# RMS norm of 16,384 rows: three loads issued from ScalarE's queue instead of SyncE's

## The chip, the cores and the metric

The kernel runs on one core of a Trainium2 chip. The metric is the device time of one execution in microseconds (us). A profile of one execution gives, beside that time, the span from the program's first instruction to its last, and says for each instruction when it ran and what it waited for. Engines are named as in the profile: PE (TensorE), DVE (VectorE), ACT (ScalarE), POOL (GpSimd) and SP (SyncE, which computes nothing and issues DMAs).

## The reference

```python
def setup_inputs():
    batch, seq, dim = 16, 1024, 512
    return {
        "x": np.random.randn(batch, seq, dim).astype(np.float32),
        "gamma": np.ones(dim, dtype=np.float32),
    }

def reference(x: np.ndarray, gamma: np.ndarray) -> np.ndarray:
    eps = 1e-5
    rms = np.sqrt(np.mean(x ** 2, axis=-1, keepdims=True) + eps)
    return (x / rms * gamma).astype(np.float32)
```

Each of the 16,384 rows of 512 numbers is divided by the root of its mean square and multiplied by gamma. 33.5 MB are read and 33.5 MB are written.

## The kernel before, in words

**Tiles and slots.** The rows are cut into four tiles (0 to 3) of 128 partitions by 32 rows by 512 numbers. A partition's 32 rows lie in one piece in memory, so that half a tile is 32 KB per partition and 4 MB in all. There are three buffers (`slots`, L40) of a whole tile each: tiles 0, 1 and 2 use slots 0, 1 and 2, and tile 3 uses slot 0 again (`slot_of`, L86), once tile 0 has been stored from it. Results are made in place.

**Groups.** Work goes by half tiles: eight groups, named by tile and first row, from (0, 0), (0, 16) to (3, 16) (L76). For each group:

- ACT squares the rows in pieces (L95) into a buffer in PSUM or SBUF, and DVE sums each piece along the row (L96). Tile 0's groups have pieces of 7 and 9 rows; the 9-row squares go to rows 23 to 31 of slot 2, which is still free. The other groups have pieces of 7, 5 and 4 rows.
- `inverse_rms`: ACT takes the square root (L101), DVE the reciprocal (L102).
- POOL multiplies the last 7 rows (6 in the first group, 3 in the last) by the reciprocal and then by gamma (L108, L109). ACT multiplies the others by the reciprocal, one instruction a row (L117), and DVE multiplies those by gamma, all in one instruction (L121).

**Order.** The order is written out by hand (`manual_schedule`, L33): every engine takes its own instructions in the order of the program. The loop at L161 runs one group ahead with the squares: while group k is scaled, the squares of group k+1 are made. In ACT's order one turn is: the next group's first two pieces of squares, the first half of this group's scalings, the third piece of squares, the second half of the scalings, what `transfers` issues, and the square root for the next group. PE only spreads gamma over the partitions at the start (L66).

**Transfers.** All DMAs are issued by SP, in the order of the program, into one queue. An issue that has to wait for something holds every issue behind it. Tile 0 (in three pieces, with gamma between), tile 1 and then tile 2's first half are loaded with no wait. `transfers` (L128), called after each group's last instruction on DVE (L175), issues the rest: tile 2's second half after group (0, 0), which has to wait for the sums of the squares kept in slot 2; after (0, 16) the two stores of tile 0, and the two loads of tile 3, each of which waits until the store of the same rows has landed; one 8 MB store of tile 1 after (1, 16), one of tile 2 after (2, 16), and two 4 MB stores of tile 3, after (3, 0) and (3, 16). `declare_no_dep` (L126) takes away waits of L121 that ACT has already made.

Of the kernel before, what the change touches and what calls it, by code (L numbers as in the profile page):

```python
# [9 lines left out]
def kernel(  # L10
# [6 lines left out]
    nc = tc.nc  # L17
# [12 lines left out]
    xv = xf.rearrange("(t p r) d -> t p r d", p=P, r=R)  # L30
# [9 lines left out]
    slots = [const.tile([P, R, D], fp32, name=f"slot{i}") for i in range(3)]  # L40

    before_scale = []

    def load(t, slot, r0, r1):
        dma = nc.sync.dma_start(out=slots[slot][:, r0:r1], in_=xv[t][:, r0:r1])  # L45
        before_scale.append((slot, r0, r1, dma))

    def store(t, slot, r0, r1):
        dma = nc.sync.dma_start(out=ov[t][:, r0:r1], in_=slots[slot][:, r0:r1])
        before_scale.append((slot, r0, r1, dma))  # L50

    gamma_row = const.tile([1, D], fp32)
    pieces = (0, D)

    load(0, 0, 0, 1)
    load(0, 0, 1, 16)
    for c0, c1 in zip(pieces, pieces[1:]):
        nc.sync.dma_start(out=gamma_row[:, c0:c1], in_=gamma.unsqueeze(0)[:, c0:c1])
    load(0, 0, 16, 32)
    load(1, 1, 0, 16)  # L60
    load(1, 1, 16, 32)
# [26 lines left out]
    def square_sums(ss, t, g, r, m, k):  # L88
        if m == 9:
            sq = slots[2][:, 23:32, :]  # L90
        else:
            home, name, most = ((psum, "sq_psum", 7), (const, "sq_sbuf", 5))[k % 2]
            sq = home.tile([P, most, D], fp32, name=name)
        rows = slots[slot_of[t]][:, g + r : g + r + m, :]
        nc.scalar.activation(out=sq[:, :m], in_=rows, func=AF.Square)  # L95
        nc.vector.tensor_reduce(  # L96
            out=ss[:, r : r + m, 0], in_=sq[:, :m], axis=mybir.AxisListType.X, op=OP.add
        )

    def inverse_rms(ss, n):  # L100
        nc.scalar.activation(out=ss[:, :n, 0], in_=ss[:, :n, 0], func=AF.Sqrt, bias=eps_t, scale=1.0 / D)  # L101
        nc.vector.reciprocal(out=ss[:, :n, 0], in_=ss[:, :n, 0])  # L102
        return ss

    def scale_by_pool(rstd, t, g, n, share):
        part = slots[slot_of[t]][:, g + n - share : g + n, :]
        by_row = rstd[:, n - share : n].to_broadcast([P, share, D])
        nc.gpsimd.tensor_tensor(out=part, in0=part, in1=by_row, op=OP.mult)  # L108
        last = nc.gpsimd.tensor_tensor(  # L109
            out=part, in0=part, in1=gamma_b.to_broadcast([P, share, D]), op=OP.mult  # L110
        )
        before_scale.append((slot_of[t], g + n - share, g + n, last))

    def scale(rstd, t, g, r0, r1):
        x = slots[slot_of[t]]
        for r in range(r0, r1):
            nc.scalar.activation(out=x[:, g + r, :], in_=x[:, g + r, :], func=AF.Copy, scale=rstd[:, r])  # L117

    def times_gamma(t, g, r0, r1):
        part = slots[slot_of[t]][:, g + r0 : g + r1, :]  # L120
        scaled = nc.vector.tensor_tensor(  # L121
            out=part, in0=part, in1=gamma_psum.to_broadcast([P, r1 - r0, D]), op=OP.mult
        )
        for slot, b0, b1, earlier in before_scale:
            if slot == slot_of[t] and b0 < g + r1 and g + r0 < b1:
                tc.declare_no_dep(scaled.ins, earlier.ins, reason="ScalarE waited for it before it scaled these rows")  # L126

    def transfers(t, g):  # L128
        if (t, g) == (0, 0):
            load(2, 2, 0, 16)  # L130
            load(2, 2, 16, 32)
        elif (t, g) == (0, 16):
            store(0, 0, 0, 16)
            store(0, 0, 16, 32)
            load(3, 0, 0, 16)
            load(3, 0, 16, 32)
        elif (t, g) == (1, 16):
            store(1, 1, 0, 32)
        elif (t, g) == (2, 16):
            store(2, 2, 0, 32)  # L140
        elif (t, g) == (3, 0):
            store(3, 0, 0, 16)
        elif (t, g) == (3, 16):
            store(3, 0, 16, 32)

    def pieces_of(group):
        t, g, n, pieces, share = group
        ss = stats.tile([P, 16, 1], fp32, name="ss")
        r = 0
        todo = []  # L150
        for k, m in enumerate(pieces):
            todo.append((ss, t, g, r, m, k))
            r += m
        return ss, todo
# [6 lines left out]
    for k, group in enumerate(groups):  # L161
        t, g, n, pieces, share = group
        mine = n - share
        half = (mine + 1) // 2
        ahead = groups[k + 1 :][:1]
        ss, todo = pieces_of(ahead[0]) if ahead else (None, [])
        scale_by_pool(rstd, t, g, n, share)
        for piece in todo[:2]:
            square_sums(*piece)
        scale(rstd, t, g, 0, half)  # L170
        for piece in todo[2:]:
            square_sums(*piece)
        scale(rstd, t, g, half, mine)
        times_gamma(t, g, 0, mine)
        transfers(t, g)  # L175
        for nxt in ahead:
            rstd = inverse_rms(ss, nxt[2])
# [30 lines left out]
```

## Time and profile before

| what | us |
|---|---|
| median of 3 runs (161.8 to 162.05) | 161.9 |
| the profiled execution, its own time | 161.72 |
| its span, first to last instruction | 159.9 |
| DVE busy, 38 instructions | 112.8 |
| ACT busy, 110 instructions | 109.1 |
| POOL busy, 22 instructions | 102.1 |
| share of 16 DMA engines' span taken by packets | 98.1% |
| mean DMA rate over the span | 420 GB/s |

The page cuts the span into 40 equal slices of 4 us and shows for each engine, and for the DMA engines together, the busy share of a slice in tenths (9 is 90% or more). A row of the order of time gives start, duration, engine, line, operation, what it writes from what it reads, and in brackets how long its engine stood idle before it and what ended that. A row of the waits gives the waiting engine and line, what it waited for, and us in total, times, and the longest; SPq is SP's sequencer, so its waits are those of the DMA queue's issues. A row of the DMA issues gives what is written from what, how often, KB each, and the median time from issue to landing.

### The profile page before, as it was taken

To read this page: it belongs to the slowest core of one execution; us is meant where nothing else is said; L and a number is where in the kernel's file an instruction comes from. 1 tells how busy PE (TensorE), PEld (TensorE's weight loads), DVE (VectorE), ACT (ScalarE), POOL (GpSimd) and SP (SyncE) were. 2 spreads that over 40 slices of the span, in tenths; PEclk is the share of its full clock that TensorE was granted. 3 is DMA by queue.
4 is the path that set the end of the run, shared out by engine and by line. 5 is a ranking of instruction groups with operands and counts; after the bars stand their busy time and mean duration, and the time that the engine had idled before them with its cause. 6 is when DMAs were issued, how large, how long until landed. Compare 5 with 4: busy or idle time off the path is not lost.

```text
span 159.9 us, 258 instructions
## 1 busy us (share of the span) xinstructions
PE 2.0 (1%) x2; PEld 0.5 (0%) x2; DVE 112.8 (71%) x38; ACT 109.1 (68%) x110; POOL 102.1 (64%) x22
## 2 busy tenths in 40 slices
PE   0005000000000000000000000000000000000000
PEld 0001000000000000000000000000000000000000
DVE  0000993797999999999999999999999702950000
ACT  3007906999998899899989989999994297000000
POOL 1000005994079999999999999999999997000000
DMA  5989999999999997999999999997997998999995
GB/s 191 492 369 468 451 393 434 484 393 418 484 410 393 483 426 311 483 393 402 508 402 393 492 426 393 524 475 311 524 459 328 524 426 361 393 459 459 393 426 229
DMA packets 2163, 67.12 MB, mean 420 GB/s; under 512 B 241, under 2 KB 241, under 8 KB 370
## 3 DMA queue, kind: packets, MB, share of 16 engines
q1 hardware_dynamic: 2162, 67.11, 98.1%
q14 instruction: 1, 0.01, 0.0%
HBM read 33.56 MB, written 33.55 MB: 420 GB/s over the span
## 4 chain that ended last, share of the span: by engine, by line
DVE 62%; ACT 18%; DMA 7%; ACTq 0%; SPq 0%; issue 0%
DVE ss L96 36%; DVE slot L121 26%; ACT slot L117 9%; DMA slot<-in_x_dram 7%; ACT slot L95 5%; ACT sq_psum L95 4%; DVE ss L102 1%; ACTq L203 0%; ACT gamma_b L160 0%; SPq L45 0%; ACT ss L101 0%; ACTq L95 0%
## 5 line engine op out<-in xcount | busy, mean ns | idle before, releaser
L108 POOL TENSOR_TENSOR slot<-slot,ss 128x3584 f32<-128x3584 f32 (+2 forms) x8 | 45.0, 5625 | 31.8 <-DVE ss L102 31.8
L96 DVE TENSOR_REDUCE ss<-sq_psum 128x7 f32<-128x3584 f32 (+1 forms) x14 | 44.5, 3176 | 19.5 <-ACT sq_psum L95 19.5
L109 POOL TENSOR_TENSOR slot<-slot,gamma_b 128x3584 f32<-128x3584 f32 (+2 forms) x8 | 56.9, 7112 | 0.6
L117 ACT ACTIVATE slot<-slot,ss 128x512 f32<-128x512 f32 x77 | 48.5, 707 | 4.9 <-DVE ss L102 4.9
L121 DVE TENSOR_TENSOR slot<-slot,gamma_psum 128x4608 f32<-128x4608 f32 (+2 forms) x8 | 42.3, 5282 | 9.3 <-ACT slot L117 9.3
L95 ACT ACTIVATE sq_psum<-slot 128x3584 f32<-128x3584 f32 (+1 forms) x14 | 36.5, 2604 | 11.4 <-DMA slot<-in_x_dram 10.4
L96 DVE TENSOR_REDUCE ss<-sq_sbuf 128x5 f32<-128x2560 f32 x6 | 16.8, 2806 | 0.0
L95 ACT ACTIVATE sq_sbuf<-slot 128x2560 f32<-128x2560 f32 x6 | 13.9, 2320 | 0.0
L96 DVE TENSOR_REDUCE ss<-slot 128x9 f32<-128x4608 f32 x2 | 9.9, 4953 | 0.1
L101 ACT ACTIVATE ss<-ss,eps_t 128x16 f32<-128x16 f32 x8 | 2.4, 306 | 8.4 <-DVE ss L96 8.4
L95 ACT ACTIVATE slot<-slot 128x4608 f32<-128x4608 f32 x2 | 8.1, 4028 | 0.0
L102 DVE RECIPROCAL ss<-ss 128x16 f32<-128x16 f32 x8 | 2.0, 249 | 0.4 <-ACT ss L101 0.4
L66 PE MATMUL gamma_psum<-gamma_row,ones_col 1*128 1x512 f32 x2 | 2.0, 1120 | 12.8 <-DMA gamma_row<-in_gamma_dram 12.8
L72 ACT ACT_TABLE_LOAD x1 | 1.3, 1283 | 1.1 <-PEq L192 1.1
L160 ACT COPY gamma_b<-gamma_psum 128x512 f32<-128x512 f32 x1 | 0.6, 566 | 0.0
L66 PEld LDWEIGHTS gamma_psum<-gamma_row,ones_col 1*128 1x128 f32 x2 | 0.5, 304 | 12.8 <-issue 12.8
L64 POOL MEMSET ones_col<- 1x128 f32 x1 | 0.2, 194 | 0.3 <-POOLq L192 0.3
L192 POOL MEMSET const-float32-0.0<- 128x1 f32 x1 | 0.1, 98 | 0.2 <-issue 0.2
L72 ACT ACTIVATE table<-eps_t 128x1 f32<-128x1 f32 x1 | 0.2, 203 | 0.0
L192 POOL MEMSET const-bfloat16-1.0<- 128x1 bf16 x1 | 0.1, 101 | 0.0
L192 POOL MEMSET const-uint8-127<- 128x1 uint8 x1 | 0.1, 101 | 0.0
L192 POOL MEMSET const-float32-1.0<- 128x1 f32 x1 | 0.1, 98 | 0.0
(1 smaller groups left out, 0.1 us busy)
## 6 DMA issues: line engine op xcount, KB each, us to landing
slot<-in_x_dram SPq DMA_DIRECT2D x7, 4096.0 KB, 27.1
out_dram<-slot SPq DMA_DIRECT2D x4, 4096.0 KB, 21.8
slot<-in_x_dram SPq DMA_DIRECT2D x1, 3840.0 KB, 11.8
slot<-in_x_dram SPq DMA_DIRECT2D x1, 256.0 KB, 3.1
out_dram<-slot SPq DMA_DIRECT2D x2, 29.2
gamma_row<-in_gamma_dram SPq DMA_DIRECT2D x1, 2.0 KB
```

The lines of the kernel that those rows point to most:

```text
L66: nc.tensor.matmul(gamma_psum[:, 0], ones_col, gamma_row, start=True, stop=True)
L72: nc.scalar.activation(out=table, in_=eps_t, func=AF.Sqrt)
L95: nc.scalar.activation(out=sq[:, :m], in_=rows, func=AF.Square)
L96: nc.vector.tensor_reduce(out=ss[:, r : r + m, 0], in_=sq[:, :m], axis=mybir.AxisListType.X, op=OP.add)
L101: nc.scalar.activation(out=ss[:, :n, 0], in_=ss[:, :n, 0], func=AF.Sqrt, bias=eps_t, scale=1.0 / D)
L102: nc.vector.reciprocal(out=ss[:, :n, 0], in_=ss[:, :n, 0])
L108: nc.gpsimd.tensor_tensor(out=part, in0=part, in1=by_row, op=OP.mult)
L109: last = nc.gpsimd.tensor_tensor(out=part, in0=part, in1=gamma_b.to_broadcast([P, share, D]), op=OP.mult)
L117: nc.scalar.activation(out=x[:, g + r, :], in_=x[:, g + r, :], func=AF.Copy, scale=rstd[:, r])
L121: scaled = nc.vector.tensor_tensor(out=part, in0=part, in1=gamma_psum.to_broadcast([P, r1 - r0, D]), op=OP.mult)
L160: nc.scalar.copy(out=gamma_b[:, 0], in_=gamma_psum[:, 0])
L192: nc = _bacc.Bacc("TRN2", target_bir_lowering=False, num_devices=1)
```

## The change

A load takes the queue to issue from as an argument. Tile 2's second half and both halves of tile 3 are issued by ACT, and all stores and the other loads still by SP. The places in the program: tile 2's second half is issued at the same call of `transfers` as before. Tile 3's first half moves from after group (0, 16) to the turn of group (1, 16), between ACT's first two pieces of squares for (2, 0) and ACT's scalings for (1, 16). Tile 3's second half moves from after group (0, 16) to after group (1, 16), so that in ACT's order it stands between the scalings of (1, 16) and the square root for (2, 0). The stores keep their order on SP, with no load between them.

```diff
-    def load(t, slot, r0, r1):
-        dma = nc.sync.dma_start(out=slots[slot][:, r0:r1], in_=xv[t][:, r0:r1])
+    def load(t, slot, r0, r1, queue=nc.sync):
+        dma = queue.dma_start(out=slots[slot][:, r0:r1], in_=xv[t][:, r0:r1])
         before_scale.append((slot, r0, r1, dma))
...
         if (t, g) == (0, 0):
             load(2, 2, 0, 16)
-            load(2, 2, 16, 32)
+            load(2, 2, 16, 32, queue=nc.scalar)
         elif (t, g) == (0, 16):
             store(0, 0, 0, 16)
             store(0, 0, 16, 32)
-            load(3, 0, 0, 16)
-            load(3, 0, 16, 32)
         elif (t, g) == (1, 16):
             store(1, 1, 0, 32)
+            load(3, 0, 16, 32, queue=nc.scalar)
...
         for piece in todo[:2]:
             square_sums(*piece)
+        if (t, g) == (1, 16):
+            load(3, 0, 0, 16, queue=nc.scalar)
         scale(rstd, t, g, 0, half)
```

## Prediction

> **What bounds the kernel now.** I read the page's engine rows and DMA line first, then the queue table, then SyncE's waits, then the landing of each transfer, then the order of time where the moved loads stand. The page:
>
> ```profile
> span 159.9 us, 258 instructions
> ...
> DVE  0000993797999999999999999999999702950000
> ACT  3007906999998899899989989999994297000000
> POOL 1000005994079999999999999999999997000000
> DMA  5989999999999997999999999997997998999995
> ...
> q1 hardware_dynamic: 2162, 67.11, 98.1%
> ```
>
> See that all traffic is in one queue (q1) and that its packets fill 98.1% of the 16 DMA engines' span, from first slice to last, while every compute engine stops some 17 to 25 us before the end. The kernel is bound by bytes. The chain of waits gives DVE 62%, but it follows compute up to 142.2 us only; the last store is ready then and lands at 159.1. SyncE's waits show the order in that queue:
>
> ```profile
> SPq L45 <- DVE ss L96: 34.1, 1, 34.1
> SPq L45 <- DMA out_dram<-slot: 22.2, 2, 12.5
> ```
>
> The second row is the two loads of tile 3, held until the stores of slot 0 have landed. The DMA issues, asked for one at a time, give issue plus time to landing. These two are the second load of tile 3 (issued 81.97) and the first store of tile 3 (issued 128.90):
>
> ```profile
> slot<-in_x_dram SPq DMA_DIRECT2D x1, 4096.0 KB, 19.1
> ```
> ```profile
> out_dram<-slot SPq DMA_DIRECT2D x1, 4096.0 KB, 20.6
> ```
>
> So they land at 101.1 and 149.5. In the same way (I write L and S for load and store, 2b for tile 2's second half, and S1, S2 for the 8 MB stores): L2a 51.8, L2b 62.2, S0a 71.9, S0b 81.95, L3a 91.3 (by its semaphore events), L3b 101.1, S1 120.4, S2 139.8, S3a 149.5, S3b 159.1. 4 MB take about 9.7 us whichever way they go, one after the other. The first packet starts 1.0 us after the first issue (0.74, 1.74), and data end about 0.4 us before a landing is seen. The packet records show each DMA engine at one packet at a time: 32 KB in 1.21 us, or 64 KB in 2.42 us for S1 and S2 (eight packets per engine and transfer).
>
> Since bytes are unchanged, the change can lose by letting the queue run dry, and gain only where the queue is idle today. **Slack of compute:** S1's data end near 119.8; S2 was issued at 114.93 and could have started at 115.9, so it has 3.9 us. S3a's data end near 149.1; S3b, issued at 142.22, could have started at 143.2: 5.9 us. The rows that matter:
>
> ```profile
> 80.75 4.95 DVE L121 TENSOR_TENSOR slot<-slot,gamma_psum 128x4608 f32<-128x4608 f32 x1
> 80.88 0.31 ACT L101 ACTIVATE ss<-ss,eps_t 128x16 f32<-128x16 f32 x1 [0.56 <-DVE ss L96]
> 81.09 3.14 ACT L95 ACTIVATE sq_psum<-slot 128x3584 f32<-128x3584 f32 x1
> ...
> 85.78 3.83 DVE L96 TENSOR_REDUCE ss<-sq_psum 128x7 f32<-128x3584 f32 x1
> 86.40 3.15 ACT L117 ACTIVATE slot<-slot,ss 128x512 f32<-128x512 f32 x5
> 86.87 6.15 POOL L108 TENSOR_TENSOR slot<-slot,ss 128x3584 f32<-128x3584 f32 x1
> ```
>
> ACT is ahead of DVE by 1.5 us (square done at 84.23, its reduction starts at 85.78), and DVE has no gap: time lost here isn't won back.
>
> **The change, part by part.**
>
> *L2b to ACT.* One issue (0.33 us on SP, L45) leaves SP at 38.01 and stands on ACT behind ten scalings that end at 39.12. Its condition, the second nine-row reduction, is met at 37.98. Behind it on ACT stands the square root at 39.03, whose reader, the reciprocal, waits for DVE until 44.56: 0.35 us is hidden. The ring then shares the engines with the rest of L1b and L2a. All three still end near 61.8, as L2a and L2b did; L2a lands up to 10 us later than before, but its first reader is the square at 67.40. Cost 0; if that cover of 5 us were gone, it would be the delay itself.
>
> *L3a to ACT.* It stands after the squares that end at 72.80 and waits for S0a (71.9). Issue 72.0 to 72.7, first packet about 73.4. What stands behind it, the scalings at 72.71, is held by at most 0.4 us, the half of which DVE hides (the scalings end at 80.31, DVE takes them at 80.75). What moves is **S0b**: alone it ran from 71.3 to 81.0; now 7.6 us of it are left at 73.4 and the engines take turns with L3a. How two rings share isn't shown by this trace. Bounds: S0b keeps all (lands 81.95) or yields all (81.0 + 9.7, landing 91.1). I take equal turns, since both have 32 KB packets and an engine holds one packet at a time: 73.4 + 15.2 = 88.6, landing 88.7 to 89.8; I use **89.2**.
>
> *L3b to ACT.* It waits for S0b's landing. On SP such a wait stood before the issue at 81.97 and held only stores that weren't ready. On ACT it stands between the scalings that end at 80.31 and the square root of 80.88, and everything behind it waits: square root, squares of 2b, scalings of 2a. From the rows' durations:
> - issue 89.2 to 89.6; square root 89.65 (+8.8); reciprocal 90.0; POOL's L108 of 2a 90.3 (before 86.87), its pair ends 104.2.
> - ACT's squares 3.1 + 2.3, scalings 3.15, square 1.9, scalings 2.54 from 89.9: ends 102.7. DVE's L121 can start there, ends 107.6; reciprocal of 2b 107.6 (before 99.30, **+8.3**).
> - POOL's L108 of 2b 107.9 (before 100.86), 14.0 us for the pair: S2 issued at **122.0** (before 114.93), first packet 123.0. The queue is dry at 119.8: **+3.2 us**.
> - Everything later on DVE is +8.3: S3b issued at 150.5, startable at 151.5. S3a now ends at 149.1 + 3.2 = 152.3: S3b loses nothing more.
>
> *When L3b lands.* It joins L3a's last two packets and S1. With turns by packet, S1's 64 KB go against 32 KB of load: a round is 2.42 + 1.21 = 3.63. Two rounds with L3a (88.3 to 95.5), six with L3b (to 117.3), then L3b's last two packets alone, to 119.7: lands **120.1**, against 101.1. Its first reader, the square before at 108.46, would otherwise be due at 108.25 + 8.3 + 0.2 = 116.8. So it starts at 120.2, and ACT again sets DVE's pace: + 12.9 as above = 133.1, L121 4.95, reciprocal at 138.1 (before 126.67), thirteen scalings 8.07 from 138.45, L121 7.09: S3b issued at **153.65**, first packet 154.65, against 152.3 when S3a ends. From its old start of 149.1 this is **+5.6 us**. It contains the 3.2; the two are one chain and are not added.
>
> *Handovers between load and store packets*, 14 in all now. Before shows: L2b before S0a took 62.2 - 51.8 = 10.4 (0.6 lost); S0b and L3a, 71.88 to 91.34, 19.46 against 19.38 (0.1); L3b before S1 about 0.1. Ends: a gain, if reading and writing overlap on an engine (the trace shows no such overlap), or 0.6 a turn. I take the nearest row, a store and a load queued together, 0.08 a pair: 1.1 us in all at most, left out of the sum and kept for the range.
>
> *SP* loses three issues, 1.0 us of a sequencer with long waits: nothing.
>
> **Sum.** The profiled execution took 161.72 (span 159.9, 1.8 around it); 161.72 + 5.6 = 167.3. The median shown, 161.9, is 0.2 above that execution: 167.5.
>
> A rule that speaks against the purpose: the page's row has SP's issues at 0.33 to 0.47 us each and DMA at 98.1%. The Trainium skill ("DMA: Bandwidth & Descriptors", section "Issuing engines are not separate DMA queues") says that issuing from several engines saves only sequencer time, for the same 16 engines do the work. By it alone the change would give about 0; it doesn't speak of the engine that has to wait before it may issue, which is my term.
>
> **The rivals.**
> 1. *Turns by bytes*, not packets: L3a ends at 92.8, L3b lands at 112.6, before 116.8. Only the dry queue before S2 is left: 161.9 + 3.2 = 165.1. For it: landings of equal sizes are very regular; against: one packet at a time.
> 2. *Dear handovers*: L3b's landing moves by 14 of them. At 0.1, 169; at 0.3, 171.6; at 0.6, 176. For it the 0.6 at 62.2, against it the two rows of 0.1.
> 3. *SP's ring first.* S0b lands at 82, but S1 (issued 86.93) then keeps L3a waiting: it lands at 110.5, and its reader of 94.78 with it. S2 is issued near 128.5, +9.7: 171.5.
> 4. *Faster: load and store packets overlap*, so that the mixed stretch moves more bytes. S0b's 15.2 us of sharing shrink by a factor r. The stall stops hurting S2 when S0b lands by 86.1 (2b's L108 then moves by 3.9), that is r = 1.26. Above it the queue gets ahead: r = 1.5 gives S2's first packet at 117.8 in place of 119.8, 159.9; the most, with no stall, 158. For it: ACT's and SP's rings never ran together before, so no row excludes it; against: both directions take the same 9.7 us, and S0b with L3a in one ring took no less than their sum.
> 5. *Nothing*: the wait on ACT doesn't hold what is behind it, and L3b lands by about 114: 161.9.
>
> **How the numbers follow.** Forecast 0.45 (166.5 to 169 by itself); rival 1 0.22; rival 2 0.12; rival 3 0.05; rival 4 0.11; rival 5 0.05. Slower: 0.45 + 0.22 + 0.12 + 0.05 = 0.84; same 0.05; faster 0.11. A measurement of this kernel can tell some 0.2% (0.3 us) from no change. The range leaves out rival 4 and the dear half of rival 2 (0.17 together): 161.8 to 171.5.
>
> **What would show it.** A second queue with 12.6 MB; S0b landing near 89; ACT idle from about 80.3 to 89.6 before L101, ended by the store's DMA; the DMA line dipping near 120 to 123 and again near 152 to 155; the first square of 3b waiting for its load until about 120; S3b issued near 153.7. Wrong if S0b lands before 86, if ACT's square root starts near 81 in spite of the wait, or if GB/s in the mixed slices rises well over 430. If L3b lands near 112, rival 1 holds.

## The result, and the profile after

The changed kernel takes 167.61 us (median of 6 runs, 167.57 to 168.7) against 161.98 (6 runs, 161.8 to 162.21). The ratio is 1.036, with a 95% interval of 1.034 to 1.038. The profiled execution took 167.58 us, its span is 165.5; before it was 161.72 and 159.9, so the two profiles differ by 5.9 in time and 5.6 in span (the last section is on the rest). The page of the changed kernel:

```profile
span 165.5 us, 258 instructions
...
DVE  0000991997999999999970889999919894069100
ACT  3008808999988999899406999997089925930000
POOL 1000007991199999999995998299999945900000
DMA  5999998999989998999989699998695996982885
...
q1 hardware_dynamic: 1730, 54.53, 77.0%
q10 hardware_dynamic: 432, 12.58, 17.8%
```

There is a second queue (q10) with 12.58 MB, the three loads of 4 MB that ACT issues. DVE, ACT and POOL now have holes in the middle and near the end, and the DMA line has dips in its last quarter. 77.0% and 17.8% make 94.8% of a longer span: the same packets, and more idle time.

The waits of ACT, longest first (us in total, times, longest), say where it stood:

```profile
ACT sq_psum L95 <- DMA slot<-in_x_dram: 15.5, 2, 10.4
ACT ss L101 <- DMA out_dram<-slot: 7.8, 1, 7.8
```

One of the two waits in the first row is the start of the kernel, 10.4 us, which was there before. The other 5.1 us and the 7.8 are new. The 7.8 in the order of time:

```profile
80.80 4.94 DVE L121 TENSOR_TENSOR slot<-slot,gamma_psum 128x4608 f32<-128x4608 f32 x1
86.98 0.33 SPq L49 DMA_DIRECT2D out_dram<-slot  x1
87.81 0.34 ACTq L45 DMA_DIRECT2D slot<-in_x_dram  x1
88.19 0.31 ACT L101 ACTIVATE ss<-ss,eps_t 128x16 f32<-128x16 f32 x1 [7.84 <-DMA out_dram<-slot]
88.41 3.14 ACT L95 ACTIVATE sq_psum<-slot 128x3584 f32<-128x3584 f32 x1
```

The ACTq row is the issue of tile 3's second half (L3b), which waited for tile 0's second store (S0b). The square root and the squares that stand behind it came 7.3 us later than before (80.88 and 81.09). The chain of work that ended last (start, us, what) names the other:

```profile
59.01 28.73 DMA out_dram<-slot
...
87.81 32.55 DMA slot<-in_x_dram
120.36 0.02 issue
120.38 3.16 ACT sq_psum L95
```

S0b lands 28.7 us after its issue (before 23.0), then L3b 32.55 us after its own (before 19.1), at 120.36, and the squares of the last group start there. Before, the chain went through DVE without a transfer in between. From 120.4 on it runs to the last store's issue at 153.54 (before 142.22). What that leaves of the DMA engines is shown by their packets that start between 150.6 and 154.2:

```profile
DMA packets 0, 0.00 MB, mean 0 GB/s; under 512 B 0, under 2 KB 0, under 8 KB 0
...
out_dram<-slot SPq DMA_DIRECT2D x1, 4096.0 KB, 11.1
```

Tile 3's first store had landed at 150.84, nothing was queued, and the last store, once issued, needs only 11.1 us (before 16.9, since it was queued ahead of time). A smaller hole lies before tile 2's store: issued at 120.39 (before 114.93), with nothing queued since the landing at 120.36.

### The profile page after: what moved, and what is told of

Same layout as the page of the kernel before. It is cut to its first block, busy times and chain, and to the rows that moved or that the text cites. A ratio compares the mean times of both kernels' runs of the same rounds, so it can differ in the third digit from the quotient of the medians.

```text
span 165.5 us, 258 instructions
## 1 busy us (share of the span) xinstructions
PE 2.0 (1%) x2; PEld 0.5 (0%) x2; DVE 113.6 (69%) x38; ACT 108.8 (66%) x110; POOL 102.2 (62%) x22
## 3 DMA queue, kind: packets, MB, share of 16 engines
q10 hardware_dynamic: 432, 12.58, 17.8%
## 4 chain that ended last, share of the span: by engine, by line
DMA 44%; ACT 25%; DVE 11%; POOL 8%; issue 4%; ACTq 0%; SPq 0%; POOLq 0%
DMA slot<-in_x_dram 27%; DMA out_dram<-slot 17%; ACT slot L117 12%; DVE slot L121 7%; ACT sq_psum L95 7%; ACT slot L95 5%; POOL slot L109 5%; POOL slot L108 4%; DVE ss L96 3%; ACT sq_sbuf L95 1%; ACTq L204 0%; ACT gamma_b L159 0%; DVE ss L102 0%; SPq L45 0%; ACT ss L101 0%
## 5 line engine op out<-in xcount | busy, mean ns | idle before, releaser
L101 ACT ACTIVATE ss<-ss,eps_t 128x16 f32<-128x16 f32 x8 | 2.4, 302 | 14.5 <-DMA out_dram<-slot 7.8
```

## The experiments

My theory was the one of the prediction: two things that L3b does, holding ACT and landing late, and of these the late landing sets the end, because 64 KB and 32 KB packets take turns. I call a queue as the DMA engines serve it a ring; SP and ACT have one each. The rivals: that two rings together move bytes more slowly (A), that issues on ACT cost ACT time (B), that the stall of ACT is the loss (C), and that the turns go by bytes. Times are compared with runs of the kernel before on the same chip; intervals are of the ratio.

**L3b from SP again, the other two loads still on ACT.**

```diff
             store(0, 0, 16, 32)
+            load(3, 0, 16, 32)
...
             store(1, 1, 0, 32)
-            load(3, 0, 16, 32, queue=nc.scalar)
```

> The changed kernel, but tile 3's second half is loaded from SP's queue again, between the second store of tile 0 and the store of tile 1; tile 2's second half and tile 3's first half stay on ACT. My theory (the loss comes from where that one load waits and from how late it lands): tile 0's second store still lands near 87.7, since it shares with tile 3's first half, but only SP waits for it. The load starts near 88.8, lands near 100, ACT does not stall, and the time is that of before, 161.9 (161.4 to 162.4). Rival A (two rings on the same engines move fewer bytes a microsecond): two rings still run together for some 45 us, so most of the loss stays, over 165. Rival B (DMA issues on ACT cost ACT time): two of the three issues stay, so two thirds of the loss, about 165.5.

161.86 us against 161.75, ratio 1.0004 (0.9993 to 1.0016). S0b still landed at 87.7, and SP waited for it. The issue of L3b at 87.69, KB and time to landing:

```profile
slot<-in_x_dram SPq DMA_DIRECT2D x1, 4096.0 KB, 13.3
```

It landed at 101.0, as before the change, and ACT's square root started on time:

```profile
80.92 0.31 ACT L101 ACTIVATE ss<-ss,eps_t 128x16 f32<-128x16 f32 x1 [0.56 <-DVE ss L96]
```

So L2b and L3a on ACT's queue, and two rings running together, cost 0.1 us by the medians and nothing within the span (159.8): A and B fall as the cause of the loss. It is L3b's.

**L3b later in ACT's order, where its condition has been met.**

```diff
             store(1, 1, 0, 32)
-            load(3, 0, 16, 32, queue=nc.scalar)
...
         scale(rstd, t, g, 0, half)
+        if (t, g) == (2, 0):
+            load(3, 0, 16, 32, queue=nc.scalar)
```

> The changed kernel, but the load of tile 3's second half stands later in ACT's order, after the first half of the scalings of group (2, 0), where its condition (tile 0's second store, landing near 87.7) has been met for some 2 us: ACT has no stall any more. My theory, by which the late landing of that load alone sets the end: it is issued near 89.6, still takes turns with the 64 KB packets of tile 1's store, lands near 120.4, the first square of group (3, 16) waits 12 us for it, the last store is issued near 153.6 and the time stays at 167.6 (167.2 to 168.6). Rival C (ACT's stall of 7.8 us is the loss): it goes with the stall, 162 to 163.5.

170.01 us, ratio 1.0507 (1.0475 to 1.054): slower than the changed kernel, though ACT's 7.8 us stall is gone. The issue was at 87.74; ACT's row of the waits and the first square of the last group:

```profile
ACT sq_psum L95 <- DMA slot<-in_x_dram: 24.6, 2, 14.3
```
```profile
122.76 3.16 ACT L95 ACTIVATE sq_psum<-slot 128x3584 f32<-128x3584 f32 x1 [14.29 <-DMA slot<-in_x_dram]
```

C falls as the whole loss: without the stall ACT merely waits 14.3 us for the load, in place of 5.1. The end came 33.2 us after the square's start in both kernels (122.76 to the last store's issue at 155.92; 120.38 to 153.54). My number was 2.4 us short, for the load landed at 122.7 and not at 120.4; the last experiment is on that.

**Tile 1's store in two transfers (32 KB packets), and in four (16 KB), the rest as in the changed kernel.**

```diff
-            store(1, 1, 0, 32)
+            store(1, 1, 0, 16)
+            store(1, 1, 16, 32)
```

> The changed kernel, but tile 1 is stored by two transfers of 16 rows in place of one of 32, so that its packets are 32 KB and not 64. My theory (rings take turns packet by packet): loads and stores now share equally, tile 3's second half lands near 112 in place of 120.4, before its first square is due at 115.2. ACT's stall stays: tile 2's store is still issued near 120.4 with the queue dry from about 119.8 to 121.4, and the time is 163.3 (162.9 to 163.8). Turns by bytes: the packet size changes nothing, 167.6. Rival C (the stall is the loss): 167.6.

```diff
-            store(1, 1, 0, 32)
+            for r in range(0, 32, 8):
+                store(1, 1, r, r + 8)
```

> The changed kernel, but tile 1 is stored by four transfers of 8 rows: packets of 16 KB. My theory: a round is one load packet of 1.21 us and one store packet of 0.61 us, so the ten load packets that are left at 87.3 take 18.2 us and tile 3's second half lands near 106. The time is the same as with two transfers, 163.3 (162.9 to 163.8), since the landing was early enough there already and only the dry queue before tile 2's store is left. Turns by bytes: landing near 120 as in the changed kernel, 167.6.

Two transfers: 163.56 us, ratio 1.0107 (1.0081 to 1.0133). Four: 163.70, 1.0115 (1.0089 to 1.0141). The queue table over a stretch in which both rings have work shows the turns (packets, MB, share of 16 engines; q1 is SP's ring, q10 ACT's). The changed kernel, 98.1 to 112.6:

```profile
DMA packets 128, 6.29 MB, mean 434 GB/s; under 512 B 0, under 2 KB 0, under 8 KB 0
...
q1 hardware_dynamic: 64, 4.19, 66.7%
q10 hardware_dynamic: 64, 2.10, 33.5%
```

Two transfers, 97.5 to 104.8:

```profile
q1 hardware_dynamic: 48, 1.57, 49.9%
q10 hardware_dynamic: 48, 1.57, 49.8%
```

Four transfers, 94.75 to 100.2:

```profile
q10 hardware_dynamic: 48, 1.57, 66.8%
q1 hardware_dynamic: 48, 0.79, 33.7%
```

Packet for packet the rings are equal, 64 to 64 and 48 to 48, and by bytes 2 to 1, 1 to 1 and 1 to 2. So turns by bytes fall. The rate of 434 GB/s is no lower than the 9.7 us for 4 MB of one ring (432). L3b landed at 114.5 and 108.0; I had said 112 and 106, for at 87.3 three packets of L3a were still to come, not two, and its completion waited for a turn as well. Both landings are early enough: with two transfers the first square of the last group starts with no wait before it, late by the stall alone:

```profile
115.23 3.14 ACT L95 ACTIVATE sq_psum<-slot 128x3584 f32<-128x3584 f32 x1
```

ACT's stall is still 7.8 us (7.7 with four), and with two transfers tile 2's store is issued at 120.47, when the queue is dry: the data before it ended at 119.9 on average and its first packet started at 121.3. The stall without the late landing costs 1.8 us (163.56 against 161.75).

**Both edits: L3b later, and tile 1 in two.**

> Both of the single edits at once: tile 3's second half issued later in ACT's order (no stall, as the run with that edit alone showed) and tile 1 stored by two transfers (32 KB packets). All three loads stay on ACT's queue. My theory: it lands near 114.5, as with the two transfers alone; its first square would be due at 108.5, so ACT waits 6 us; from the start of that square to the issue of the last store the changed kernel took 33.2 us, so the last store is issued near 147.7, just inside the 148.1 that the queue allows: 161.9 (161.5 to 162.4), the time of before. If the two rings or ACT's issues cost anything by themselves, it shows here: over 163.

162.10 us against 161.74, ratio 1.0027 (1.0017 to 1.0037). The first square and the last store's issue:

```profile
114.25 3.16 ACT L95 ACTIVATE sq_psum<-slot 128x3584 f32<-128x3584 f32 x1 [5.76 <-DMA slot<-in_x_dram]
```
```profile
147.43 0.33 SPq L49 DMA_DIRECT2D out_dram<-slot  x1
```

All three loads are on ACT's queue, and all but 0.36 us of the loss is gone, with the last store issued 5.2 us later than before: it is still in time for the queue. The remaining 0.36 us lies outside the span, which is 159.9 as before: these runs took 2.08 to 2.17 us more than their spans, those of the kernel before on the same chip 1.73 to 1.83.

**Control: the kernel before with tile 1 in two.** The edit is the one of two transfers above, on the kernel before.

> A control: the kernel before, with tile 1 stored by two transfers of 16 rows. One ring only, so packet size decides no turns; the extra issue on SP (0.34 us) lies under a full queue, and tile 1's first half can't go out sooner than the transfers ahead of it. My theory: 161.9, no change (161.5 to 162.3). If splitting the store saves time by itself, the gain of the two runs with a split store is partly that: then 161 or less here.

161.85 us against 161.74, ratio 1.0011 (1.0003 to 1.0020). The split by itself saves nothing; it costs 0.1 us if anything. What it saves in the changed kernel is the turns.

**L3b later, and tile 2's store in four (16 KB packets).** On top of the second experiment:

```diff
-            store(2, 2, 0, 32)
+            for r in range(0, 32, 8):
+                store(2, 2, r, r + 8)
```

> The kernel with the load issued later in ACT's order, which took 170.0, and in addition tile 2 stored by four transfers of 8 rows (16 KB packets in place of 64 KB). In that run the load's last data packet ended near 119.7, as in the changed kernel, but its landing was seen at 122.7, after the first 64 KB packet (2.42 us) of tile 2's store, which was already queued. My theory: the completion signal is a packet of its own and waits for a turn; behind a 16 KB packet (0.61 us) the landing is seen near 120.9, 1.8 us sooner, and the time falls from 170.0 to 168.2 (167.8 to 168.6). Rival: the late landing has to do with the stall's absence or the load's later issue, not with tile 2's packets: 170.0 again.

168.53 us, ratio 1.045 (1.0411 to 1.0489) against 170.01 and 1.0507 (not on the same chip). In the profiles the last store is issued at 154.06 in place of 155.92. The first square of the last group:

```profile
120.90 3.16 ACT L95 ACTIVATE sq_psum<-slot 128x3584 f32<-128x3584 f32 x1 [12.42 <-DMA slot<-in_x_dram]
```

The load is seen 1.86 us sooner than behind 64 KB packets (122.76), by the difference of 2.42 and 0.61. The packet records say why: the 4-byte packets that signal L3b's landing ran at 119.6 to 120.1 in the changed kernel, where the other ring was empty, at 121.8 to 122.4 behind the 64 KB packet (all but one of the 16), and at 120.1 to 120.5 here, while the last data packet ended at 119.7 on average in all three. The one exception among the 16 fits: by the times, on that DMA engine the other ring's turn went to the 4-byte signal of tile 1's store, at 119.72, and L3b's signal followed at once. So the late landing is a turn that the signal waited for.

## Why the prediction was right, point by point

It said 167.5, and 167.6 was measured. The sum's +5.6 is the difference of the spans. The close hit hides a term: the 1.8 us around the span were taken as unchanged, and were 2.1. For the profiled execution the sum gave 167.3, and 167.58 was measured; that the medians agree to 0.1 is in part luck. The steps:

- **Bound by bytes, no gain to be had: right.** In the runs in which no hole opens, the time is that of before within 0.3%, with one ring or two. The rule weighed there, that issuing from several engines saves only sequencer time, agrees with the first experiment (1.0004), in which no issue holds ACT up.
- **L2b at no cost: right.** It was issued at 38.06 and landed with L2a, 62.5 and 62.3; L2a's first square started at 67.44.
- **L3a's issue, right; its first packet, wrong by 2.7 us.** Issued at 72.11, it had its first packet at 76.05 and not at 73.4: two more of S0b's packets went first. So S0b landed at **87.73** in place of 89.2. No row of before had a transfer start on an empty ring beside a busy one; I had used the 1.0 us of the kernel's very first load.
- **ACT's wait holds what stands behind it: right.** The square root came 7.3 us later and I had 8.8, too much by S0b's 1.5; the idle time before it was 7.84 us.
- **Tile 2's store late with the queue dry: right in kind, mis-sized.** 120.39 in place of 122.0, and the hole alone is worth 1.8 us of the median in place of 3.2. The error is S0b's 1.5 again, for everything on that path counts from its landing. Rival 1, turns by bytes, was priced with this term: with equal turns it would have been 163.6, not 165.1.
- **L3b's landing: right, 120.36 against 120.1.** The way there was not quite the predicted one: L3a's last three packets went with no store between them, tile 1's store shared with L3b, and only L3b's last packet ran alone. The landing didn't inherit these errors: with two packets' worth of store for one of load, L3b is the last thing to end of all that was queued then. The engines had not run dry, so those bytes end at 119.8 whenever S0b lands. Turns by packet were an assumption of the prediction; the experiments with 64, 32 and 16 KB show them, and so does the changed kernel. The Trainium skill ("DMA: Bandwidth & Descriptors", section "Queues, rings and completion order") says the same, that an engine goes round its rings packet by packet.
- **The rest of the chain: right, 153.54 against 153.65 for the last store's issue**, and no handover cost. The two terms were said to be one chain and not to be added; that the stall alone can be taken away without any gain shows it. I had not seen that it would even lose: with no hole before tile 2's store, that store is there to take the turn before L3b's signal.
- **Rivals 2, 3, 4 and 5** show nowhere. The mixed stretch moved 434 GB/s, so handovers are not dear (2) and nothing overlaps (4); S0b was slowed by 5.8 us, so SP's ring is not served first (3); and the wait on ACT is plain in the trace (5). The 0.6 us that spoke for rival 2 were misread: in the kernel before they lie in L2b's own last two packets on each DMA engine (1.35 and 1.92 us on average in place of 1.21), before the store's first packet there. Why these are slow isn't shown.

## What to carry to other kernels

In this kernel, whose DMA engines are full, a second queue added no bytes a microsecond (434 against 432 GB/s). It decided whose bytes go first, and a load that shared with a store of larger packets got the smaller share. So ask for each load early enough for its reader at that share, and where that can't be, make the store's packets smaller. Put an issue that must wait for a landing on an engine with nothing behind it, and place it in a busy engine's order only after the point where its condition holds. And before a stall is removed, follow what comes after it: here it was hidden behind a later arrival, and taking it away alone bought nothing.

## What the runs showed of the hardware that I had not expected

- A transfer issued to an empty ring while the other ring is busy can start late, but not by a fixed time. In the changed kernel L3a's first packet came 3.9 us after its issue (72.11, 76.05) and tile 1's store's 3.6 us after (86.98, 90.57), each after three 32 KB packets of the other ring. With tile 1's store in two, its first packet came 1.2 us after the issue (87.02, 88.21), after one. On idle engines it was 1.0 us for the kernel's first load and 0.8 for tile 2's store (120.39, 121.22). What sets the delay isn't shown.
- The signal of a landing takes a turn of its own. It ran up to 2.4 us after the data behind a 64 KB packet, 0.6 behind a 16 KB packet. By the Trainium skill (the same page and section) the completion increment is a strongly ordered write, which lands after all earlier writes of that DMA engine, across its queues; the trace agrees that another queue's packet can stand before it, and the records of the 4-byte packets show the delay already in when they start.
- Load and store packets in alternation lost nothing: 128 packets in 14.5 us at 434 GB/s.
- The time outside the span was longer with a second ring in use. Every run with loads on ACT's queue took 1.98 to 2.17 us more than its span, and every run with SP's queue alone whose span is on record 1.73 to 1.83. What takes that time isn't shown.
